# Weaving two chunks of each weight tile column by column, so that TensorE loads its weights with a step of two

## The chip, the cores and the metric

The kernel runs on one core of a Trainium2 chip. The metric is the time of one execution in device microseconds; the number quoted for a kernel is the median of its runs. Beside the timed runs there is one profiled execution, whose trace gives every instruction's start, duration and engine; all durations below come from that one.

## What is computed

Two layers (DEPTH = 2) of a diffusion backbone work on 256 latent tokens and 256 context tokens of width 1024. A layer is a half-step SwiGLU feed-forward block, a token mixer (neighbourhood attention, a recurrent unit and a Fourier mix behind one input projection, and one output projection), and a second feed-forward block. Each is modulated by vectors made from `silu(c) @ w_ada`, and followed by a residual and a LayerNorm. Cut to what matters here:

```python
def swiglu(h, wg, wu, wd):
    return (jax.nn.silu(h @ wg) * (h @ wu)) @ wd

def ffn_sublayer(xs, m, j, wg, wu, wd, g, b):
    y = MACARON * swiglu(modulate(xs, m, j), wg, wu, wd)
    return residual_post_norm(xs, m[3 * j + 2] * y, g, b)

# token mixing: one projection in, three head groups, one projection out
q, k, v, xr, gr, f = jnp.split(h_lat @ w_in, cuts, axis=-1)
y_lat = jnp.concatenate([na_lat, lru_lat, fno_lat], axis=-1) @ w_out
```

All of it is float32. Nearly all of the arithmetic is `h @ weight`: gate and up projections of 1024 x 2816, the down projection of 2816 x 1024 (twice in a layer), the projections in and out of the mixer.

## The kernel before

**The products.** Activations stand transposed: 128 channels on the partitions, 512 tokens (256 context, 256 latent) along the free dimension. A matmul holds a 128 x 128 block of weights in the array and streams 256 tokens past it. For float32 accuracy from the faster `float32r` format every operand is split in two: a rounded high part and the rest as a low part. A product is then three matmuls: high weights times high activations, low weights times high, high weights times low. In the names, `whi` and `wlo` are the two parts of a weight tile; `hH`, `hL` and `aH`, `aL` those of the activations.

**A weight unit.** The weights come in units of 128 output columns and up to 8 chunks of 128 input rows. A unit is one tile of 128 partitions and 1024 columns, chunk after chunk: column `k * 128 + s` is output column `s` of chunk `k`. A down projection is cut into groups of 8, 7 and 7 chunks (`GROUPS`), so its second and third group have units of 7 chunks, 896 columns. The DMA that SyncE issues fills `raw` (5 buffers), ScalarE (ACT) rounds `raw` to `whi` in one copy (`use_one`, line 274), and VectorE (DVE), or GpSimd (POOL) for a listed part of the units, writes `wlo = raw - whi` (`split_lo`, line 591). `whi` and `wlo` have 5 buffers each. The last units before a norm go another way: in `later` they are kept as four quarters of 256 columns, and each quarter is split when there is room (in `piece` at line 637 and in `norm_latent` at line 660).

**The matmuls.** `proj_start` (lines 402 to 436) walks over the chunks: for chunk `k` it takes the block `kk_(h_, k)` of `whi` and `kk_(l_, k)` of `wlo`, 128 neighbouring columns each, and calls `mmh` (line 391), which issues one matmul for each 256 tokens. Every matmul instruction loads its own weights, so the trace has one weight load (LDWEIGHTS, on the row PEld) for each matmul (on PE), and the load for the next one runs while the present one streams:

```python
def kk_(t, k):
    return t[:, k * 128:(k + 1) * 128]
```

**What sets the order.** `advance` splits units ahead of their use (`LOOK = 5`), in one fixed order for the whole program; DVE also does the adaLN products (`acc`, lines 298 to 304), the residuals, the norms and parts of the attention. In the mixer the order is a list written out by hand (`ORDER`). The tiny matmuls `adat` (line 332) turn the adaLN sums into columns between two units of a feed-forward block.

Of the kernel before, what the change touches and what calls it, by code (L numbers as in the profile page):

```python
# [65 lines left out]
def kernel(ctx: ExitStack, tc: tile.TileContext, x, cx, vecs, cst, bias, w_ada,  # L66
# [15 lines left out]
    V, S, G, PE = nc.vector, nc.scalar, nc.gpsimd, nc.tensor  # L82
# [65 lines left out]
    for l in range(DEPTH):  # L148
        p = {}
# [66 lines left out]
    later = []  # L216
    lazy = object()
# [42 lines left out]
    def needs_ctx(l, b):  # L260
        return l == 0 or b < 10

    def use_one(eng=None):
        i = ptr["use"]
        it = seq[i]
        t = raw.pop(i)
        if it[0] in "bx":
            kept[it] = t
        elif it[0] == "w":
            n = units[it[1]][1] * 128  # L270
            h_ = whi_p.tile([128, 1024], F32R, tag="whi", name="whi")
            l_ = wlo_p.tile([128, 1024], F32R, tag="wlo", name="wlo")
            if eng is not lazy:
                S.copy(h_[:, :n], t[:, :n])  # L274
            if eng is None and it[1] in pool_lo:
                eng = G
            if eng is later or eng is lazy:
                for a, b in ((q * n // 4, (q + 1) * n // 4) for q in range(4)):
                    later.append((l_[:, a:b], t[:, a:b], h_[:, a:b], G) + (eng is lazy) * (0,))
            else:  # L280
                split_lo(l_[:, :n], t[:, :n], h_[:, :n], eng)
            hi[it[1]], lo[it[1]] = h_, l_
        elif it[0] == "a":
            _, l, b, kp = it
            nst = 2 if needs_ctx(l, b) else 1
            if kp == 0:
                acc[l, b] = acc_p.tile([128, 2, 512], F32, tag="acc", name="acc")
            a = acc[l, b]
            half = [slice(0, 64), slice(64, 128)]
            if kp == 3 and nst == 2:  # L290
                acc[l, b] = acc_p.tile([128, 2, 512], F32, tag="acc", name="fold")
            for kk in range(2):
                k = kp * 2 + kk
                for st in range(nst):
                    sc_ = scol[:, k, st:st + 1]
                    if k == KD - 1 and nst == 2:
                        for i, p in enumerate(half):
                            V.scalar_tensor_tensor(out=acc[l, b][half[st], i], in0=t[p, 512:], scalar=sc_[p],  # L298
                                                   in1=a[p, st], op0=ALU.mult, op1=ALU.add)
                        continue  # L300
                    if k == 0:
                        V.tensor_scalar(out=a[:, st], in0=t[:, :512], scalar1=sc_, scalar2=None, op0=ALU.mult)
                    else:
                        V.scalar_tensor_tensor(out=a[:, st], in0=t[:, kk * 512:(kk + 1) * 512], scalar=sc_,  # L304
                                               in1=a[:, st], op0=ALU.mult, op1=ALU.add)
            if kp == 3:
                pend_red.append([l, b, 0, None])
        else:
            _, l, b, kp = it
            if kp == 0:  # L310
                acc[l, b] = dps("adap")

            for kk in range(2):
                k = kp * 2 + kk
                PE.matmul(acc[l, b][32 * (k % 4):32 * (k % 4) + 32, :], lhsT=scol_z[:, k, :],
                          rhs=t[:, kk * 512:(kk + 1) * 512], start=(k < 4), stop=(k >= 4))
            if kp == 3 and l:
                pend_rows.append([l, b, None])
        ptr["use"] += 1
        if not own_room(it):  # L320
            ptr["raw"] -= 1
        issue()
# [67 lines left out]
        for i, c in enumerate(halves):  # L390
            PE.matmul(o[:, c], lhsT=w, rhs=X[:, k, c], start=first and i == 0, stop=last and i == len(halves) - 1)  # L391

    def kk_(t, k):
        return t[:, k * 128:(k + 1) * 128]


    def proj(us, tiles, X, c0, c1, order=None):
# [4 lines left out]
    def proj_start(us, tiles, X, late_w=False):  # L402
# [4 lines left out]
        def go(ks, c0, c1, i0=0, i1=len(us)):  # L407
            c = [slice(a, min(a + 256, c1)) for a in range(c0, c1, 256)]
            for k in ks:
                if late_w:  # L410
                    for i, ((h_, l_), o) in list(enumerate(zip(ws, tiles)))[i0:i1]:
                        n = done[c0, i] = done.get((c0, i), 0) + 1
                        mmh(o, kk_(h_, k), X[0], k, c, n == 1, False)
                        mmh(o, kk_(h_, k), X[1], k, c, False, False)
                        mmh(o, kk_(l_, k), X[0], k, c, False, n == nk)
                    continue
                high(k, c0, c1)
                low(k, c0, c1)

        def high(k, c0, c1):  # L420

            c = [slice(a, min(a + 256, c1)) for a in range(c0, c1, 256)]
            n = done[c0, "h"] = done.get((c0, "h"), 0) + 1
            for (h_, l_), o in zip(ws, tiles):
                mmh(o, kk_(h_, k), X[0], k, c, n == 1, False)
                mmh(o, kk_(l_, k), X[0], k, c, False, False)

        def low(k, c0, c1):
            c = [slice(a, min(a + 256, c1)) for a in range(c0, c1, 256)]
            n = done[c0, "l"] = done.get((c0, "l"), 0) + 1  # L430
            assert n <= done[c0, "h"]
            for (h_, l_), o in zip(ws, tiles):
                mmh(o, kk_(h_, k), X[1], k, c, False, n == nk)

        go.high, go.low = high, low
        return go
# [974 lines left out]
```

## Time and profile before

| what | value |
|---|---|
| runs shown | 1807.26, 1807.67, 1811.6 us; median 1807.67 us |
| the profiled execution's own time | 1805.85 us |
| its span, first to last instruction | 1804.1 us |
| mean granted clock of TensorE | 0.982 |
| PE busy | 1722.3 us, 95% of the span, 14241 matmuls |
| PEld busy (weight loads) | 1667.0 us, 92%, 14241 loads |
| DVE, ACT, POOL busy | 1227.6 us (68%), 699.9 us (39%), 324.7 us (18%) |

How to read it: PE busy is the time in which some matmul was under way. Matmuls are pipelined, so one matmul's duration (some 280 ns) is much longer than the distance from its start to the next one's start (some 115 ns). That distance is called the *pace* below. A busy PE can therefore still become quicker, if its pace falls; and what the pace is, is read from the count of matmuls in a stretch or from their starting times, never from the durations.

### The profile page before, as it was taken

The page shows a single profiled execution, that of the slowest core. Times are in us where ns is not written, and L with a number is a line of the kernel's source. Part 1 is how long each engine was busy: PE and PEld are TensorE (multiplying, and loading weights), DVE is VectorE, ACT ScalarE, POOL GpSimd, SP SyncE. Part 2 cuts the span into 40 slices and gives each one's busy share as a digit, 9 for nine tenths or more (in the row PEclk, how much of TensorE's full clock was granted, in tenths as well). Part 3 has the DMA queues.
Part 4 walks back from the last instruction along what each step waited for, and adds up shares of the span by engine and source line. Part 5 has one row for each costly group of instructions (what it writes and reads, how often), then busy time and mean ns, then how long its engine had stood idle before and what let it go on. Part 6 is the DMA issues. An engine that isn't in the chain of part 4 may idle for free.

```text
span 1804.1 us, 33865 instructions
## 1 busy us (share of the span) xinstructions
PE 1722.3 (95%) x14241; PEld 1667.0 (92%) x14241; DVE 1227.6 (68%) x1867; ACT 699.9 (39%) x1119; POOL 324.7 (18%) x258
## 2 busy tenths in 40 slices
PE   7999999998899999999999999999999988979997
PEld 5999999998788999999999999999999967869997
DVE  3799899847586488765664568855653768676565
ACT  2222222225756554312222363222222566655443
POOL 0132121215441062000000140000000556150000
PEclk9999999999999999999999999999999989989998
DMA  8565555632223125544444326565653233267662
GB/s 274 181 205 179 168 172 171 175 96 83 68 62 93 55 86 172 176 141 138 132 146 123 95 70 197 168 186 169 181 173 89 81 94 88 89 177 205 181 196 84
DMA packets 375080, 253.33 MB, mean 140 GB/s; under 512 B 8144, under 2 KB 336336, under 8 KB 374928
## 3 DMA queue, kind: packets, MB, share of 16 engines
q1 hardware_dynamic: 373856, 248.81, 46.6%
q8 instruction: 112, 1.84, 0.4%
q0 software_dynamic: 1072, 2.36, 0.4%
q14 instruction: 40, 0.33, 0.1%
HBM read 250.09 MB, written 1.05 MB: 139 GB/s over the span
## 4 chain that ended last, share of the span: by engine, by line
PE 76%; DVE 16%; ACT 4%; issue 3%; DMA 0%; POOL 0%; SPq 0%; DVEq 0%; ACTq 0%
PE gu L391 41%; PE dn L391 19%; PE head L391 5%; PE pj L391 3%; DVE acc L304 2%; PE wo L391 2%; PE adat L332 1%; DVE wlo L591 1%; DVE ri L903 1%; PE o L1097 1%; DVE xT L718 1%; DVE s L460 1%; DVE xl L870 1%; DVE fold L298 1%; ACT whi L274 1%
## 5 line engine op out<-in xcount | busy, mean ns | idle before, releaser
L391 PE MATMUL gu<-hH,whi 128*128 128x256 f32 x2336 | 494.7, 281 | 1.8 <-ACT hH L1262 1.8
L391 PE MATMUL gu<-hH,wlo 128*128 128x256 f32 x2336 | 491.7, 280 | 1.7 <-DVE wlo L591 1.7
L391 PE MATMUL gu<-hL,whi 128*128 128x256 f32 x2336 | 492.1, 280 | 1.0 <-DVE hL L591 0.9
L274 ACT CAST whi<-raw 128x1024 fp32r<-128x1024 f32 (+1 forms) x319 | 319.1, 1025 | 273.4 <-PE dn L391 97.6
L591 POOL TENSOR_TENSOR wlo<-raw,whi 128x1024 fp32r<-128x1024 f32 (+2 forms) x106 | 204.2, 1933 | 1174.8 <-ACT whi L274 1154.3
L391 PEld LDWEIGHTS gu<-hH,whi 128*128 128x128 f32 x2336 | 371.9, 190 | 5.7 <-ACT hH L1262 2.4
L391 PEld LDWEIGHTS gu<-hL,whi 128*128 128x128 f32 x2336 | 370.8, 190 | 1.6 <-DVE hL L591 1.6
L391 PEld LDWEIGHTS gu<-hH,wlo 128*128 128x128 f32 x2336 | 370.0, 189 | 2.2 <-DVE wlo L591 2.2
L591 DVE TENSOR_TENSOR wlo<-raw,whi 128x1024 fp32r<-128x1024 f32 (+1 forms) x245 | 297.7, 1218 | 92.2 <-ACT whi L274 89.3
L391 PE MATMUL dn<-aH,whi 128*128 128x256 f32 x1280 | 283.5, 281 | 1.6 <-DVE xT L718 1.6
L391 PE MATMUL dn<-aL,whi 128*128 128x256 f32 x1280 | 281.0, 279 | 0.0
L391 PE MATMUL dn<-aH,wlo 128*128 128x256 f32 x1280 | 280.8, 279 | 0.0
L304 DVE SCALAR_TENSOR_TENSOR acc<-raw,scol,acc 128x512 f32<-128x512 f32 x337 | 273.9, 860 | 1.0
L731 ACT CAST aH<-pr 128x512 fp32r<-128x512 f32 (+1 forms) x88 | 50.0, 568 | 420.8 <-DVE pr L730 420.8
L391 PEld LDWEIGHTS dn<-aH,whi 128*128 128x128 f32 x1280 | 207.5, 189 | 2.1 <-DVE xT L718 2.0
L391 PEld LDWEIGHTS dn<-aL,whi 128*128 128x128 f32 x1280 | 207.7, 189 | 0.0
L391 PEld LDWEIGHTS dn<-aH,wlo 128*128 128x128 f32 x1280 | 207.1, 188 | 0.1
L730 DVE TENSOR_TENSOR pr<-sg,gu 128x512 f32<-128x512 f32 (+1 forms) x84 | 51.6, 614 | 136.9 <-PE gu L391 131.9
L718 DVE SCALAR_TENSOR_TENSOR xT<-dn,gate,xT 128x256 f32<-128x256 f32 x174 | 78.0, 478 | 82.8 <-PE dn L391 82.4
L391 PE MATMUL pj<-hH,whi 128*128 128x256 f32 x384 | 84.0, 287 | 5.5 <-ACT pt L1066 2.8
L729 ACT ACTIVATE sg<-gu 128x512 f32<-128x512 f32 (+1 forms) x84 | 45.2, 538 | 107.5 <-PE gu L391 107.3
L391 PE MATMUL pj<-hH,wlo 128*128 128x256 f32 x384 | 82.7, 283 | 0.0
(239 smaller groups left out, 2129.0 us busy)
## 6 DMA issues: line engine op xcount, KB each, us to landing
raw<-in_w_ada_dram SPq DMA_DIRECT2D x136, 512.0 KB, 4.7
raw<-in_ff_gate_dram SPq DMA_DIRECT2D x88, 512.0 KB, 4.4
raw<-in_ff_up_dram SPq DMA_DIRECT2D x88, 512.0 KB, 4.8
raw<-in_ff_down_dram SPq DMA_DIRECT2D x64, 448.0 KB, 4.4
raw<-in_w_in_dram SPq DMA_DIRECT2D x36, 512.0 KB, 3.9
raw<-in_ff_down_dram SPq DMA_DIRECT2D x32, 512.0 KB, 4.7
raw<-in_w_out_dram SPq DMA_DIRECT2D x16, 512.0 KB, 4.1
in<-in_w_ada_dram SPq DMA_DIRECT2D x8, 512.0 KB, 6.9
```

The costliest lines, as they stand in the source:

```text
L274: S.copy(h_[:, :n], t[:, :n])
L298: V.scalar_tensor_tensor(out=acc[l, b][half[st], i], in0=t[p, 512:], scalar=sc_[p], in1=a[p, st], op0=ALU.mult, op1=ALU.add)
L304: V.scalar_tensor_tensor(out=a[:, st], in0=t[:, kk * 512:(kk + 1) * 512], scalar=sc_, in1=a[:, st], op0=ALU.mult, op1=ALU.add)
L332: PE.matmul(tp[:, q * 2:q * 2 + 2], lhsT=a[:, q * 128:(q + 1) * 128], rhs=w, start=True, stop=True)
L391: PE.matmul(o[:, c], lhsT=w, rhs=X[:, k, c], start=first and i == 0, stop=last and i == len(halves) - 1)
L460: (e1 or V).tensor_tensor(out=s1, in0=a, in1=z, op=ALU.add)
L591: (eng or V).tensor_tensor(out=dst_l, in0=src, in1=dst_h.bitcast(F32), op=ALU.subtract)
L718: V.scalar_tensor_tensor(out=xT[:, j, a:b], in0=ps[:, a:b], scalar=gate[:, st, j:j + 1], in1=xT[:, j, a:b], op0=ALU.mult, op1=ALU.add)
L729: S.activation(out=sg[:, c], in_=gp[:, c], func=AF.Silu)
L730: V.tensor_tensor(out=pr[:, c], in0=sg[:, c], in1=up[:, c], op=ALU.mult)
L731: S.copy(aH[:, m, c], pr[:, c])
L870: V.scalar_tensor_tensor(out=t3[:, :, off:], in0=s3[:, :, :256 - off], scalar=w[tp], in1=t3[:, :, off:], op0=ALU.mult, op1=ALU.add)
```

## The change

`in_order` and `woven` view 256 columns of a tile (two chunks `t = 0, 1` of 128 columns `s`) in two ways: with the two chunks one after the other, as `raw` has them, and with their columns alternating. `whi` and `wlo` are written through the second view, so that column `s` of chunk `2j + t` stands at `256 j + 2 s + t`. The DMA and `raw` stay as they are; ACT, DVE and POOL write (and DVE and POOL also read `whi`) with a step of two elements. `kk_` then takes every second column of a pair: 128 columns with a step of two, which reach over 1024 bytes of a partition instead of 512. A unit of 7 chunks has an odd chunk left; it keeps its 128 neighbouring columns, and it is copied and split by an instruction of its own (`in_pieces` gives two pieces, of 768 and 128 columns).

```diff
+    def in_order(t, a, b):
+        return t[:, a:b].rearrange("p (k t s) -> p k t s", t=2, s=128)
+
+    def woven(t, a, b):
+
+        return t[:, a:b].rearrange("p (k s t) -> p k t s", t=2, s=128)
+
+    def in_pieces(n):
+
+        e = n // 256 * 256
+        out = [(lambda t: in_order(t, 0, e), lambda t: woven(t, 0, e))]
+        if e < n:
+            out.append((lambda t: t[:, e:n],) * 2)
+        return out
+
     def use_one(eng=None):
...
             if eng is not lazy:
-                S.copy(h_[:, :n], t[:, :n])
+                for src, dst in in_pieces(n):
+                    S.copy(dst(h_), src(t))
...
                 for a, b in ((q * n // 4, (q + 1) * n // 4) for q in range(4)):
-                    later.append((l_[:, a:b], t[:, a:b], h_[:, a:b], G) + (eng is lazy) * (0,))
+                    later.append((woven(l_, a, b), in_order(t, a, b), woven(h_, a, b), G) + (eng is lazy) * (0,))
             else:
-                split_lo(l_[:, :n], t[:, :n], h_[:, :n], eng)
+                for src, dst in in_pieces(n):
+                    split_lo(dst(l_), src(t), dst(h_), eng)
...
-    def kk_(t, k):
-        return t[:, k * 128:(k + 1) * 128]
+    def kk_(t, k, nk):
+        if k == nk - 1 and nk % 2:
+            return t[:, k * 128:(k + 1) * 128]
+        return t[:, k // 2 * 256:(k // 2 + 1) * 256].rearrange("p (s t) -> p t s", t=2)[:, k % 2]
...
-                        mmh(o, kk_(h_, k), X[0], k, c, n == 1, False)
-                        mmh(o, kk_(h_, k), X[1], k, c, False, False)
-                        mmh(o, kk_(l_, k), X[0], k, c, False, n == nk)
+                        mmh(o, kk_(h_, k, nk), X[0], k, c, n == 1, False)
+                        mmh(o, kk_(h_, k, nk), X[1], k, c, False, False)
+                        mmh(o, kk_(l_, k, nk), X[0], k, c, False, n == nk)
```

`high` and `low` pass `nk` in the same way. The order of the work on every engine stays; 64 copies on ACT, 54 subtractions on DVE and 10 on POOL come in, one for each unit of 7 chunks. On ACT, at the end of the first feed-forward block's second group of gate and up projections (`sg` and `aH` are that block's activation, `whi` the weights' high part), there stood before:

```order
50 L729 ACTIVATE sg<-gu 128x512
51 L731 CAST aH<-pr 128x512
52 L274 CAST whi<-raw 128x1024 x2
53 L729 ACTIVATE sg<-gu 128x512
54 L731 CAST aH<-pr 128x512
55 L274 CAST whi<-raw 128x1024
56 L274 CAST whi<-raw 128x896
57 L729 ACTIVATE sg<-gu 128x512
```

and there stands now:

```order
50 L748 ACTIVATE sg<-gu 128x512
51 L750 CAST aH<-pr 128x512
52 L290 CAST whi<-raw 128x4x2x128 x2
53 L748 ACTIVATE sg<-gu 128x512
54 L750 CAST aH<-pr 128x512
55 L290 CAST whi<-raw 128x4x2x128
56 L290 CAST whi<-raw 128x3x2x128
57 L290 CAST whi<-raw 128x128
58 L748 ACTIVATE sg<-gu 128x512
```

Every copy of a whole unit has become one woven copy; the copy of 896 columns has become two. On DVE, in the same block between the adaLN products (`acc`, `fold`) and the product of the gate (`pr`), there stood before:

```order
187 L298 SCALAR_TENSOR_TENSOR fold<-raw,scol,acc 64x512 x4
188 L591 TENSOR_TENSOR wlo<-raw,whi 128x896
189 L325 TENSOR_TENSOR mcol_105<-adat,vT 128x2x4
190 L730 TENSOR_TENSOR pr<-sg,gu 128x512
191 L1211 TENSOR_SCALAR k_r<-k_r 128x8
```

and there stands now:

```order
187 L315 SCALAR_TENSOR_TENSOR fold<-raw,scol,acc 64x512 x4
188 L610 TENSOR_TENSOR wlo<-raw,whi 128x3x2x128
189 L610 TENSOR_TENSOR wlo<-raw,whi 128x128
190 L342 TENSOR_TENSOR mcol_105<-adat,vT 128x2x4
191 L749 TENSOR_TENSOR pr<-sg,gu 128x512
192 L1230 TENSOR_SCALAR k_r<-k_r 128x8
```

One subtraction has become two, and nothing else has moved. The line numbers are 16 to 19 higher in the changed kernel.

## Rows read from the trace of the kernel before

**Rows 1.** Page: busy time, share of the span and instructions of each engine.

```profile
PE 1722.3 (95%) x14241; PEld 1667.0 (92%) x14241; DVE 1227.6 (68%) x1867; ACT 699.9 (39%) x1119; POOL 324.7 (18%) x258
```

**Rows 2.** Page: the chain that ended last, its shares by engine.

```profile
PE 76%; DVE 16%; ACT 4%; issue 3%; DMA 0%; POOL 0%; SPq 0%; DVEq 0%; ACTq 0%
```

**Rows 3.** Users of `whi`: count, duration ns min/median/max, first and last start, forms.

```profile
L391 PEld LDWEIGHTS gu<-hH,whi x2336: 186/188/338, 29.4 to 1769.8; 128*128 128x128 f32 x195
L391 PE MATMUL gu<-hH,whi x2336: 276/281/583, 29.4 to 1770.0; 128*128 128x256 f32 x195
...
L391 PE MATMUL dn<-aH,whi x1280: 276/281/471, 140.9 to 1790.6; 128*128 128x256 f32 x183
...
L391 PE MATMUL pj<-hH,whi x384: 276/278/550, 460.5 to 1555.2; 128*128 128x256 f32 x192
...
L391 PE MATMUL head<-hH,whi x256: 276/281/579, 435.9 to 1452.3; 128*128 128x256 f32 x128
...
L391 PE MATMUL wo<-aH,whi x144: 276/281/388, 602.1 to 1590.4; 128*128 128x256 f32 x144
```

**Rows 4.** Groups, 1627 to 1770 us: busy us, mean ns of one | idle before.

```profile
L391 PE MATMUL gu<-hH,whi 128*128 128x256 f32 x302 | 83.4, 276 | 0.0
L391 PEld LDWEIGHTS gu<-hH,whi 128*128 128x128 f32 x301 | 56.5, 188 | 0.0
```

**Rows 5.** The same groups, 811 to 866 us.

```profile
L391 PE MATMUL gu<-hH,whi 128*128 128x256 f32 x156 | 31.1, 281 | 0.0
L391 PEld LDWEIGHTS gu<-hH,whi 128*128 128x128 f32 x156 | 24.1, 190 | 0.0
```

**Rows 6.** Stretches, L391 alone: length, PE busy (x), PEld busy (x), clock, DMA share, GB/s.

```profile
811.00:866.00 55.00, 55.00 (x469) 55.00 (x469) 1.00 0.46 139
...
1627.00:1770.00 143.00, 143.00 (x1264) 143.00 (x1264) 1.00 0.66 191
```

**Rows 7.** Timeline of PEld: start us, us, instruction, count.

```profile
366.23 0.97 PEld L332 LDWEIGHTS adat<-pick,fold 128*128 128x128 f32 x8
```

**Rows 8.** Timeline of PE: eight records of transposes of `xT`.

```profile
1539.05 1.03 PE L1064 MATMUL ptp<-cs,xT 128*128 128x128 f32 x8
```

**Rows 9.** Timeline of PE: score matmuls with 512 streamed columns.

```profile
1467.84 0.39 PE L1005 MATMUL sc<-k,q 128*128 128x512 f32 x1
1468.07 0.39 PE L1006 MATMUL sc<-k,q 128*128 128x512 f32 x1
1468.30 0.39 PE L1005 MATMUL sc<-k,q 128*128 128x512 f32 x1
```

**Rows 10.** Groups by form, whole span: the splitting of weights, and two shorter subtractions.

```profile
L274 ACT CAST whi<-raw 128x1024 fp32r<-128x1024 f32 x255 | 260.8, 1047 | 235.3 <-PE dn L391 93.7 <-DMA raw<-in_ff_gate_dram 54.2 <-DMA raw<-in_ff_down_dram 31.6
L591 DVE TENSOR_TENSOR wlo<-raw,whi 128x1024 fp32r<-128x1024 f32 x191 | 236.4, 1241 | 71.8 <-ACT whi L274 69.3 <-issue 2.0
...
L274 ACT CAST whi<-raw 128x896 fp32r<-128x896 f32 x64 | 58.9, 940 | 38.1 <-DMA raw<-in_ff_down_dram 28.0 <-PE dn L391 3.9 <-PE adat L332 3.1
...
L591 DVE TENSOR_TENSOR aL<-pr,aH 128x512 fp32r<-128x512 f32 x66 | 45.0, 686 | 6.3 <-ACT aH L731 6.2
...
L591 DVE TENSOR_TENSOR aL<-pr,aH 128x256 fp32r<-128x256 f32 x22 | 9.2, 420 | 1.6 <-ACT aH L731 1.4
...
L591 POOL TENSOR_TENSOR wlo<-raw,whi 128x1024 fp32r<-128x1024 f32 x60 | 153.3, 2564 | 425.1 <-ACT whi L274 404.6 <-DVE mod L575 8.7 <-DVE k_r L1209 8.5
...
L591 POOL TENSOR_TENSOR wlo<-raw,whi 128x256 fp32r<-128x256 f32 x36 | 28.5, 798 | 7.0 <-ACT whi L274 7.0
```

**Rows 11.** Groups on DVE: one reads with a step of two, one without.

```profile
L325 DVE TENSOR_TENSOR mcol<-adat,vT 128x8 f32<-128x8 f32 x32 | 5.2, 163 | 89.1 <-PE adat L332 89.1
...
L1209 DVE TENSOR_TENSOR k_r<-k_r,k_z 128x8 f32<-128x8 f32 x8 | 1.3, 168 | 0.3
```

**Rows 12.** Stretch of the fullest DVE: length, PE, PEld, DVE, ACT, POOL, clock, DMA.

```profile
60.00:240.00 180.00, 176.47 (x1505) 175.90 (x1504) 162.91 (x237) 45.77 (x56) 44.16 (x25) 0.99 0.60 179
```

**Rows 13.** The same stretch, users of `wlo` alone: PE, PEld, DVE, POOL.

```profile
60.00:240.00 180.00, 96.60 (x486) 74.44 (x486) 22.81 (x17) 37.78 (x14) 0.99 0.60 179
```

More of the change, by code (lines that the diff above doesn't have):

```diff
@@ L424, in high @@
             for (h_, l_), o in zip(ws, tiles):
-                mmh(o, kk_(h_, k), X[0], k, c, n == 1, False)
-                mmh(o, kk_(l_, k), X[0], k, c, False, False)
+                mmh(o, kk_(h_, k, nk), X[0], k, c, n == 1, False)
+                mmh(o, kk_(l_, k, nk), X[0], k, c, False, False)
         def low(k, c0, c1):
@@ L432, in low @@
             for (h_, l_), o in zip(ws, tiles):
-                mmh(o, kk_(h_, k), X[1], k, c, False, n == nk)
+                mmh(o, kk_(h_, k, nk), X[1], k, c, False, n == nk)
         go.high, go.low = high, low
```

## The prediction

> **What bounds the kernel now.** I read the busy table first. PE has a matmul under way for 1722.3 of 1804.1 us [rows 1], so only some 82 us of the span are free of matmuls. The chain that ended last agrees: 76% of it is PE, 16% DVE, 4% ACT [rows 2]. So the time is the number of matmuls times their pace, plus a little waiting for DVE and ACT.
>
> The number comes from the users of `whi`. Each of the five products has three matmul groups of equal count (high-high, low-high, high-low), of which the high-high row is shown: 3 x (2336 + 1280 + 384 + 256 + 144) = 13,200 matmuls on line 391 [rows 3]. Those are the ones that the change touches. One nanosecond of their pace is 13.2 us, 0.7% of the time.
>
> The pace is read from stretches without a break. Between 1627 and 1770 us there are 1264 matmuls in 143 us; with the two or three that the edges cut taken off, that is 113.3 ns each. Between 811 and 866 us there are 469 in 55 us, 117.8 ns each in the same way [rows 6]. [...] It is the same instruction, of the same shape; its recorded duration is 276 ns in the fast stretch [rows 4] and 281 ns in the slow one [rows 5], so the duration tells which pace a matmul ran at. For `gu`, `dn`, `head` and `wo` the median is 281, for `pj` 278 [rows 3]: a little over half run at the slow pace. I take 52%, a mean pace of 0.52 x 117.8 + 0.48 x 113.3 = 115.6 ns.
>
> The weight loads differ too: 188 ns in the fast stretch, 190 ns on average in the slow one [rows 4, 5]. Something makes loads and matmuls late together.
>
> **How near the weight load is to the bound.** Eight loads in a row for the tiny `adat` matmuls, which stream two columns only, take 0.97 us; taking off one load's 0.19, (0.97 - 0.19) / 7 = 111 to 112 ns from load to load [rows 7]. So the load alone would hold the pace at about 112 ns: the fast pace is one nanosecond above it. The transposes, plain fp32 instructions with a load each, show what is possible below that: (1.03 - 0.27) / 7 = 109 ns [rows 8], the 0.27 being their duration.
>
> **The change part by part.** (1) *The load with a step of two.* The trace has no such load, so I bound its effect by the nearest rows. Gain: the lowest pace of any full matmul here is 109 ns [rows 8], so at most 13,200 x (115.6 - 109) = 87 us. Loss: if the load has to fetch twice as much and the part that grows with the columns doubles, 112 ns become up to 224, and 13,200 x (224 - 115.6) = 1.43 ms come on top. No row excludes that. I take a value at the gain's end, near the fast pace, for this reason. There are two stable paces for the same work at the same clock, the slow one with loads that are late as well: the two streams of reads of TensorE (256 columns of activations, 1024 bytes of each partition, and 128 columns of weights, 512 bytes) disturb each other. They go through memory in the same time, so now the activations' addresses move twice as fast as the weights'. With a step of two the 128 weights reach over 1024 bytes also, and the two streams move alike; two streams at one speed need not meet again and again. I expect the slow pace to go, and what is left to lie between the load's own 112 and the fast 113.3: 112.7 ns. That gives 13,200 x (115.6 - 112.7) = 38 us.
>
> (2) *Weaving on ACT, DVE and POOL.* From 1024 and 896 columns, 1047 and 940 ns, a copy on ACT costs 0.84 ns for each column and 0.19 us besides; 64 more copies are 12 us of an engine that is 39% busy [rows 1, 10]. On DVE, 512 and 256 columns at 686 and 420 ns give 0.15 us besides [rows 10]: 54 x 0.15 = 8 us. On POOL, 1024 and 256 columns at 2564 and 798 ns give 0.2 us: 10 x 0.2 = 2 us, 18% busy. PE's matmuls cover ACT and POOL altogether, since units are split up to five ahead. DVE has little room only from 60 to 240 us, 162.9 of 180 us busy [rows 12]; I charge 2 us for what comes through there and in the norms. Whether steps of two make these engines slower for each column is not shown at size: the one row in which DVE reads with a step of two has 8 elements, 163 ns against 168 without [rows 11], which speaks for no cost, and I take none. Bound: if every column cost twice as much, the 17 subtractions of that stretch, 22.8 us now [rows 13], would take some 18 us more, and DVE would need 181 us of 180; so up to 20 us could come through there. In the other direction these engines can't gain: they do the same columns in the same or more instructions.
>
> (3) *Waits.* None is added. A matmul of an even chunk waits for the piece with its pair, which is at most as large as the whole unit was; the odd chunk waits for an instruction behind it, and it is the last to be used. DMAs and their order stay. If PE becomes 38 us faster, weights are wanted 2% sooner: the stretch from 60 to 240 us has 1505 matmuls, would lose 4 us, and DVE's 163 us still fit into 176.
>
> Sum, against the profiled execution: 1805.85 - 38 + 2 = 1770 us. The runs' median is 1.8 us (0.1%) above that execution; I leave it there. No change means within 0.3%, 5.4 us, about what a measurement of this kernel can tell.
>
> **The rivals.** *A. Nothing changes on PE.* The two paces could belong to the stream of activations alone. [...] Against it speaks that the loads of the slow stretch are late too [rows 4, 5]. Time: 1805.85 + 2 = 1808.
>
> [...]
>
> *B. More goes than the slow pace.* If the excess of both paces comes from the two streams, and the load's 112 comes from the same source, the pace falls to 109: 1805.85 - 87 + 2 = 1721 us. For it: plain fp32 instructions run at 109 beside their loads. [...]
>
> *C. The load becomes the bound (slower).* The load is the mechanism, on PEld, under every one of the 13,200 matmuls. Its 112 ns have 1.3 ns of room under the fast pace; every nanosecond more than that is exposed. With a step of two a load reaches over twice as many bytes. If it becomes 5 ns slower, nearly the step between the two paces, it comes to 117 and every matmul runs at the slow pace or a little above, 117.8: 13,200 x (117.8 - 115.6) = 29 us, with the 2 us of weaving 1837 us. From 3.6 ns on (112 to 115.6) the change is a loss. For it: the small room. Against it: nothing in the trace shows a step to cost anything, at 8 elements. The far end of the load's bound, more than 3 ms, belongs here too.
>
> [...]
>
> That the change doesn't do what it says can be left out: the 128 columns of a load are the same values in either layout, and each matmul loads its own.
>
> **How the numbers follow.** Forecast 0.34, A 0.20, B 0.17, C 0.29 (of which 0.05 for the far end and 0.05 for weaving that costs more than I took). Faster by over 0.3%: forecast and B, 0.51. Within 0.3%: 0.20. Slower: 0.29. The time is the forecast's, 1770. The range goes from B, with a few microseconds below it, 1715, to C, 1840: it leaves out the far end and half of what is left of C above it, about 0.12, and 0.05 below. The forecast's own range, paces of 112 to 113.3 with 0 to 4 us of weaving, is 1758 to 1780.
>
> **What would show it.** Right: line-408 matmuls with one duration only, 276 ns or less, in all stretches; some 488 starts in an unbroken 55 us where there were 469; 128-column pieces of 0.3 us on ACT and DVE; ACT's woven copies at 1047 ns and DVE's at 1241. Rival A: 276 and 281 still side by side. B: durations near 272, a pace of 109. C: loads longer than 192 ns in long unbroken stretches. It would be wrong above all if the step changes the pace in a way that neither of the present two paces shows.

## The result, and the profile after

The changed kernel takes 1854.28 us (median of 4 runs, 1852.91 to 1854.96) against 1807.47 us (4 runs): a ratio of 1.0256, 95% interval [1.0234, 1.0277]. It is 2.6% slower. The prediction was 1770 us with a range to 1840, so both its sign and its range failed.

The busy table and the chain's shares of the profile after, the profiled execution of 1854.79 us with a span of 1853.0:

```profile
PE 1777.2 (96%) x14241; PEld 1723.3 (93%) x14241; DVE 1231.9 (66%) x1921; ACT 731.9 (40%) x1183; POOL 333.7 (18%) x268
PE 79%; DVE 14%; ACT 3%; issue 3%; DMA 1%; SPq 0%; DVEq 0%; ACTq 0%
```

The count of matmuls is that of [rows 1], and PE is busy 54.9 us longer. The time free of matmuls fell from 81.8 to 75.8 us. So nothing waits longer than before: all of the loss, and 6 us more, is in the pace of the matmuls themselves, on the engine on which the chain lies.

Stretches of the profile after, line 408 alone; the columns are those of [rows 6]:

```profile
831.00:887.00 56.00, 56.00 (x470) 56.00 (x468) 1.00 0.46 137
1666.00:1823.00 157.00, 157.00 (x1311) 157.00 (x1310) 1.00 0.62 179
```

With the two or three that the edges cut taken off, that is 119.9 ns from start to start in both, at a granted clock of 1.00, as there. The stretch that ran at 113.3 in [rows 6] and the one that ran at 117.8 now run alike, and slower than either. Averaged over every two starts on that line that are less than 140 ns apart (some 12,880), the pace went from 115.7 to 119.9 ns; times 13,200 that is 55 us, about what PE's busy time gained.

The groups by form that answer to [rows 3, 10], whole span (busy us, mean ns of one | idle before):

```profile
L408 PE MATMUL gu<-hH,whi 128*128 128x256 f32 x2336 | 504.1, 285 | 1.9 <-ACT hH L1281 1.8
L408 PEld LDWEIGHTS gu<-hH,whi 128*128 128x128 f32 x2336 | 382.7, 196 | 5.8 <-ACT hH L1281 2.5 <-issue 1.7 <-ACT hH L622 1.7
...
L290 ACT CAST whi<-raw 128x1024 fp32r<-128x1024 f32 x255 | 284.6, 1143 | 236.7 <-PE dn L408 96.3 <-DMA raw<-in_ff_gate_dram 45.1 <-DMA raw<-in_ff_down_dram 30.6
...
L290 ACT CAST whi<-raw 128x128 fp32r<-128x128 f32 x64 | 18.9, 295 | 0.0
...
L610 DVE TENSOR_TENSOR wlo<-raw,whi 128x1024 fp32r<-128x1024 f32 x191 | 236.4, 1241 | 77.4 <-ACT whi L290 74.5 <-issue 2.4
...
L610 DVE TENSOR_TENSOR wlo<-raw,whi 128x128 fp32r<-128x128 f32 x54 | 15.6, 289 | 0.0
```

The mean weight load is now 196 ns over the whole span. In the stretch from 831 to 887 us it is 194, where the slow stretch of before had 190 [rows 5]:

```profile
L408 PEld LDWEIGHTS gu<-hH,whi 128*128 128x128 f32 x156 | 24.3, 194 | 0.0
```

ACT's woven copy takes 1143 ns where the straight one took 1047 [rows 10]; DVE's subtraction takes 1241 in either layout, and POOL's 2609 where it took 2564. The last chunk of an odd unit goes in pieces of 0.3 us on ACT and DVE.

### The profile page after: what moved, and what is told of

Its sections match the earlier page's. It is cut to its first block, busy times and chain, and to the rows that moved or that the text cites. A ratio compares the mean times of both kernels' runs of the same rounds, so it can differ in the third digit from the quotient of the medians.

```text
span 1853.0 us, 33996 instructions
## 1 busy us (share of the span) xinstructions
PE 1777.2 (96%) x14241; PEld 1723.3 (93%) x14241; DVE 1231.9 (66%) x1921; ACT 731.9 (40%) x1183; POOL 333.7 (18%) x268
## 4 chain that ended last, share of the span: by engine, by line
PE 79%; DVE 14%; ACT 3%; issue 3%; DMA 1%; SPq 0%; DVEq 0%; ACTq 0%
PE gu L408 41%; PE dn L408 21%; PE head L408 5%; PE pj L408 3%; PE wo L408 2%; DVE acc L321 2%; PE adat L349 1%; DVE ri L922 1%; PE o L1116 1%; DVE s L479 1%; DVE wlo L610 1%; DVE xT L737 1%; ACT whi L290 1%; PE gate L898 1%; DVE xl L889 1%
## 5 line engine op out<-in xcount | busy, mean ns | idle before, releaser
L408 PE MATMUL gu<-hH,whi 128*128 128x256 f32 x2336 | 504.1, 285 | 1.9 <-ACT hH L1281 1.8
L408 PE MATMUL gu<-hH,wlo 128*128 128x256 f32 x2336 | 500.3, 283 | 2.0 <-DVE wlo L610 2.0
L408 PE MATMUL gu<-hL,whi 128*128 128x256 f32 x2336 | 500.6, 283 | 1.2 <-DVE hL L610 1.1
L290 ACT CAST whi<-raw 128x1024 fp32r<-128x1024 f32 (+2 forms) x383 | 352.0, 962 | 273.1 <-PE dn L408 100.8
L610 POOL TENSOR_TENSOR wlo<-raw,whi 128x1024 fp32r<-128x1024 f32 (+3 forms) x116 | 213.7, 1852 | 1203.3 <-ACT whi L290 1155.2
L408 PEld LDWEIGHTS gu<-hH,whi 128*128 128x128 f32 x2336 | 382.7, 196 | 5.8 <-ACT hH L1281 2.5
L408 PEld LDWEIGHTS gu<-hH,wlo 128*128 128x128 f32 x2336 | 382.7, 195 | 2.4 <-DVE wlo L610 2.4
L408 PEld LDWEIGHTS gu<-hL,whi 128*128 128x128 f32 x2336 | 383.2, 196 | 1.7 <-DVE hL L610 1.7
L610 DVE TENSOR_TENSOR wlo<-raw,whi 128x1024 fp32r<-128x1024 f32 (+2 forms) x299 | 301.5, 1025 | 97.3 <-ACT whi L290 93.9
L408 PEld LDWEIGHTS dn<-aH,wlo 128*128 128x128 f32 x1280 | 213.7, 194 | 0.1
```

What stands on the lines that cost most here:

```text
L290: S.copy(dst(h_), src(t))
L610: (eng or V).tensor_tensor(out=dst_l, in0=src, in1=dst_h.bitcast(F32), op=ALU.subtract)
```

## The experiments

Kernels that consist of blocks of matmuls, and nothing of the reference, are called benches. In a bench `W` holds the weights, `X` the stream, and the 256-column blocks go to X's two halves in turn, as the kernel does.

**Reading alone, and weaving alone.** Two kernels take the change apart. The first is the kernel before with the new loads and no weaving, so that each product mixes the columns of two neighbouring chunks:

```diff
-    def kk_(t, k):
-        return t[:, k * 128:(k + 1) * 128]
+    def kk_(t, k, nk):
+        if k == nk - 1 and nk % 2:
+            return t[:, k * 128:(k + 1) * 128]
+        return t[:, k // 2 * 256:(k // 2 + 1) * 256].rearrange("p (s t) -> p t s", t=2)[:, k % 2]
```

> The kernel before with the loads' step of two alone: the tiles are not woven, so each load takes every second column of a pair of neighbouring chunks (the products mix two chunks' weights; order and amount of work are unchanged). If the step of the loads makes the whole difference: 1852 to 1856 us, pace 120.0 in unbroken stretches. If weaving has a part of the 47 us: 1807.5 plus the rest, for instance 1840 if ACT's 100 ns more for each copy come through.

Measured: 1850.78 us, ratio 1.0238 [1.0218, 1.0258]. The second is the changed kernel with that function put back, so that the tiles are woven and the loads straight (its products, too, mix the columns of two chunks):

> The changed kernel with loads of 128 neighbouring columns again: the tiles are woven by ACT, DVE and POOL as in the change, but read straight (the products take the wrong columns; the amount of work is unchanged). If the step of the loads makes the whole difference: 1805 to 1810 us, paces of 113 and 118 side by side as before. If weaving costs time: over 1813 us, with longer waits of PE for whi and wlo.

Measured: 1809.21 us, ratio 1.0009 [0.9998, 1.002]. One unbroken stretch of the first and two of the second, their products' line alone:

```profile
1666.00:1822.00 156.00, 156.00 (x1303) 156.00 (x1303) 1.00 0.62 180
```

```profile
894.00:950.00 56.00, 56.00 (x496) 56.00 (x495) 1.00 0.53 161
1625.00:1778.00 153.00, 153.00 (x1301) 153.00 (x1300) 1.00 0.64 184
```

Reading with a step gives the 120 ns of the changed kernel (156 / 1301). Weaving alone keeps the two paces of before, 113.3 and 117.8, though not in the same stretches: the long one that was fast is now slow. The loads' step makes the loss, within the two intervals; weaving is hidden.

**The load's step in a bench.** Blocks of 96 matmuls, in which the step of the weights and the streamed columns differ:

```python
if step == 1:
    w = W[:, k * 128:k * 128 + cols]
else:
    b = (k // step) * 128 * step % 1024
    w = W[:, b:b + cols * step].rearrange("p (s t) -> p t s", t=step)[:, k % step]
```

> A kernel of its own: nothing but blocks of 96 float32r matmuls from one tile of weights and one of activations, each block with another step of the weights (1, 2, 3, 4, 8), width of the weights (128, 64, 32 columns), number of streamed columns (16, 256, 384, 512) and step of the streamed columns (1, 2); it leaves out the whole of the reference. Three theories. [...] (2) The load is the bound: the pace with 16 streamed columns, where nothing else takes time, is 112 at step one and 120 at step two, and at 384 and 512 streamed columns the step changes nothing. (3) The stream has its own excess: with 64 or 32 weight columns the pace at 256 stays 113 or more, and at 512 it is 226 or more whatever the step; step two then adds something that isn't in the stream.

The timeline of PE, start us and us (the digits at a name's end are left out by the trace: w1, w2 and so on is the step, the shape tells the streamed columns):

```profile
26.41 11.68 PE L56 MATMUL w1n<-X,W 128*128 128x256 f32 x96
37.93 11.68 PE L56 MATMUL w2n<-X,W 128*128 128x256 f32 x96
49.45 17.15 PE L56 MATMUL w3n<-X,W 128*128 128x256 f32 x96
66.44 22.57 PE L56 MATMUL w4n<-X,W 128*128 128x256 f32 x96
88.85 23.33 PE L56 MATMUL w8n<-X,W 128*128 128x256 f32 x96
112.01 21.95 PE L56 MATMUL w1n<-X,W 128*128 128x512 f32 x96
133.80 22.57 PE L56 MATMUL w2n<-X,W 128*128 128x512 f32 x96
...
272.76 16.81 PE L56 MATMUL w1n<-X,W 128*128 128x384 f32 x96
289.40 16.80 PE L56 MATMUL w2n<-X,W 128*128 128x384 f32 x96
```

From start to start of two blocks, by 96: step one 120.0, two 120.0, three 177, four 233, eight 241 ns. So the load does pay for its step, steeply from three on, where the pace is far above the 120.0 of straight loads behind the same 256 columns. But at 256 columns straight loads ran at 120.0 as well, a third pace that no long unbroken stretch of before had, so the bench did not repeat the 113.3 and could not price a step of two. Behind 384 columns the two steps are equal, 173.3; behind 512 they are not: 227.0 without a step and 233.3 with one, although PEld is idle for part of the time there (busy for 36.40 of 44 us from 112 to 156, over the two blocks). So a longer stream does not hide the step in every case.

Two of the blocks with straight loads of only 32 columns, which take 108 ns each on average (those of 128 columns 192):

```profile
250.60 11.06 PE L56 MATMUL w1c32n<-X,W 128*32 128x256 f32 x96
...
438.61 11.47 PE L56 MATMUL w1c32n<-X,W 128*32 128x256 f32 x96
```

They ran at 113.3 and at 117.8 ns, the two paces of the kernel before. So neither pace needs a load of 128 columns, and 256 streamed columns took 113.3 ns even beside a load a quarter as wide. The blocks of 16 columns, meant to show the load alone, fell to a granted clock of 0.50 and said nothing: a miss.

**The load alone.** The same in shorter blocks between wide ones, at a granted clock of 1.00, and blocks in which the weights begin some columns further:

```python
SHORT = [(f"s{s}n{n}y", s, n, 16, "W", 0) for n in (16, 64, 128, 192, 224) for s in (1, 2, 4)]
```

> A second kernel of blocks of matmuls (the reference is left out whole). Four plain fp32 matmuls of two columns, like adat, stand as a break before each block of 256 or 512 streamed columns, ten times for step one and step two; short blocks of 16 matmuls with 16 to 224 streamed columns stand between full ones, so that the clock stays up; the last blocks take weights from a tile 64 KB further off, or from 1 to 32 columns later. Theory of two streams: a load with a step of two has no room left in its reading, and the activations' stream hardly any, so that they disturb each other only while both run: with 64 or 128 streamed columns step one and step two both take about 112 ns, at 256 step two takes 120 and step one 113, 118 or 120 by the phase that the break leaves, at 512 it is 227 against 233, at 320 the step makes 0 to 7 ns. Rival, the load alone is the bound: at 64 and 128 streamed columns step two takes 120 ns, and at 320, 448 and 512 the step makes no difference. Rival, the memory's place: blocks with the far tile or a later first column have another pace than those of the same step at the old place.

The timeline of PEld (16 loads, behind 16 and 128 streamed columns), then that of PE behind 320 columns and with the weights 1, 2, 4 and 16 columns on (`o1`, `o2`, `o4`, `o16`):

```profile
304.96 1.88 PEld L62 LDWEIGHTS s1n16y<-X,W 128*128 128x128 f32 x16
312.50 1.96 PEld L62 LDWEIGHTS s2n16y<-X,W 128*128 128x128 f32 x16
320.13 3.81 PEld L62 LDWEIGHTS s4n16y<-X,W 128*128 128x128 f32 x16
...
356.97 1.88 PEld L62 LDWEIGHTS s1n128y<-X,W 128*128 128x128 f32 x16
364.51 1.97 PEld L62 LDWEIGHTS s2n128y<-X,W 128*128 128x128 f32 x16
```

```profile
567.12 5.92 PE L62 MATMUL s1n256o1z<-X,W 128*128 128x256 f32 x48
573.69 5.80 PE L62 MATMUL s1n256o2z<-X,W 128*128 128x256 f32 x48
580.14 5.92 PE L62 MATMUL s1n256o4z<-X,W 128*128 128x256 f32 x48
...
593.28 5.71 PE L62 MATMUL s1n256o16z<-X,W 128*128 128x256 f32 x48
...
637.71 7.28 PE L62 MATMUL s1n320z<-X,W 128*128 128x320 f32 x48
645.64 7.29 PE L62 MATMUL s2n320z<-X,W 128*128 128x320 f32 x48
```

Taking off one load's mean duration (192 ns for step one, 196 for two, 329 for four) and dividing by 15, a load follows a load after 112.5 ns with a step of one, 117.6 with two, 232 with four. Behind 16 streamed columns there is next to no stream to meet, and behind 128 it is the same: these are the load's own rates. The step of two costs 5 ns by itself, and the load with it needs more than the 115.6 ns of the mean matmul before. Behind 320 columns the step costs next to nothing (7.28 and 7.29 us for 48 matmuls). A load that has become too long for 256 columns is rival C's mechanism. The `o` blocks brought something else: one and the same straight load runs at 118.3, 115.6 or 113.3 ns as its place moves (5.71 against 5.92 us of 48 matmuls).

The same bench moved the weights with a step of two as well, by 4, 8 and 32 columns:

```profile
606.22 5.95 PE L62 MATMUL s2n256o4z<-X,W 128*128 128x256 f32 x48
...
619.47 6.06 PE L62 MATMUL s2n256o32z<-X,W 128*128 128x256 f32 x48
```

By the starts inside the blocks these are 118.6, 120.0 and 121.1 ns. So the pace with a step of two moves with the place too, and here stays above the 117.6 of the load alone.

**Wider matmuls.** If the load is the bound only because 256 columns are just as long, one matmul of 512 columns per load hides it. The kernel before and the changed one, with

```diff
-            c = [slice(a, min(a + 256, c1)) for a in range(c0, c1, 256)]
+            c = [slice(a, min(a + 512, c1)) for a in range(c0, c1, 512)]
```

in all three places:

> The kernel before with one matmul of 512 streamed columns where there were two of 256 (where both token streams are projected at once), so half of the loads there, each with 128 neighbouring columns. By the blocks measured before, 226.7 ns for 512 columns against a mean of 2 x 115.6 = 231.2: with some 5,000 pairs 20 to 25 us less, 1780 to 1788 us. If the excess belongs to the stream alone and its phase, as the score matmuls' 226 to 236 ns would have it, the mean stays at 231 and the time at 1800 to 1808.

> The changed kernel with one matmul of 512 streamed columns where there were two of 256. Theory of two streams: 233.3 ns for 512 columns, which is less than 2 x 120.0 but over the 226.7 of step one: 6.7 ns more than the kernel with wide matmuls and straight loads in each of some 5,000, that is 30 to 35 us above it plus what the 256-column matmuls keep of the loss (4.4 ns in each of some 3,000, 13 us). If the load alone is the bound, it is hidden behind 512 columns, and only the 256-column matmuls lose: 10 to 15 us above it.

Measured: 1814.57 us, ratio 1.004 [1.0026, 1.0055], and 1813.95 us, 1.0034 [1.0022, 1.0046]. A stretch of 512-column matmuls in either (PE, PEld):

```profile
898.00:955.00 57.00, 57.00 (x246) 45.94 (x245) 1.00 0.54 157
```

```profile
893.00:949.00 56.00, 56.00 (x244) 47.17 (x243) 1.00 0.53 159
```

With half the loads, the loads no longer fill PEld (46 of 57 us), and the changed kernel is no slower than the other. Both expectations are misses, however. The kernel before with wide matmuls gains nothing: a 512-column matmul takes some 233 ns without a step (57 / 244.5), where twice 113.3 would be 226.7. The streamed columns have an excess of their own, which fewer loads don't remove. And the changed kernel, expected at least 10 us above it, lies level, though not because the step is simply hidden. Some 3,200 matmuls still have 256 columns, since only one of the two token streams is projected there, and in the changed kernel they still pay for it; its longest stretch of them ran at 119.9 ns, where the kernel before with wide matmuls ran at 117.8:

```profile
1626.00:1782.00 156.00, 156.00 (x1303) 156.00 (x1303) 1.00 0.63 180
```

Over the whole traces the 256-column matmuls go at 119.9 against 116.3 ns, some 12 us lost, and the 4,900 wide ones at 230.4 against 233.3, some 14 us gained; the two cancel. Behind 512 columns the step gained 3 ns in the kernel and cost 6 in the bench, and no run shows why.

**Place or phase.** One thing differs from block to block: the column at which the weights begin (w), the stream's (x), or a lone narrow matmul that shifts the first load against the first stream (p behind weight column 0, q behind column 16):

```python
CASES = [(f"w{w}o", 1, w, 0, 0) for w in (0, 8, 16, 24, 32, 48, 64, 96, 112, 128, 256, 272)]
CASES += [(f"x{x}o", 1, 0, x, 0) for x in (4, 16, 32, 48, 64)]
CASES += [(f"p{p}o", 1, 0, 0, p) for p in (6, 20, 50, 78, 110, 140)]
CASES += [(f"q{p}o", 1, 16, 0, p) for p in (6, 20, 50, 78, 110, 140)]
```

> Blocks of 64 matmuls of 256 streamed columns, each behind a pause; one thing differs from block to block: the column at which the weights begin (w0 to w272), the column at which the stream begins (x4 to x64), a lone matmul of 6 to 140 columns ahead that shifts the start of the first load against the first stream (p at weight column 0, q at weight column 16), all with a step of one; and with a step of two the lone matmul (r) and the weight column (t). It computes nothing of the reference. The block at weight column 0 went at 120 ns in the run before and the one at column 16 at 113.3. Theory (places): the pace of straight loads is set by where weights and stream lie: all p at 120, all q at 113.3, and moving the stream by 16 columns against the weights gives 113.3 as moving the weights did. Rival (phase): it is set by how far the load has got when the stream starts, and kept: the p and q blocks spread over 113.3, 117.8 and 120 whatever the column. Both: a load with a step of two never goes below 117.6 (its floor behind 16 streamed columns), so every r and t block lies between 117.6 and 121.

Timeline of PE (64 matmuls of 256 columns each):

```profile
46.31 7.92 PE L55 MATMUL w0o<-X,W 128*128 128x256 f32 x64
...
63.35 7.78 PE L55 MATMUL w16o<-X,W 128*128 128x256 f32 x64
...
80.19 7.83 PE L55 MATMUL w32o<-X,W 128*128 128x256 f32 x64
...
97.10 7.92 PE L55 MATMUL w64o<-X,W 128*128 128x256 f32 x64
...
156.66 7.78 PE L55 MATMUL x16o<-X,W 128*128 128x256 f32 x64
165.09 7.84 PE L55 MATMUL x32o<-X,W 128*128 128x256 f32 x64
...
242.75 7.52 PE L55 MATMUL q6o<-X,W 128*128 128x256 f32 x64
...
251.03 7.79 PE L55 MATMUL q20o<-X,W 128*128 128x256 f32 x64
```

From the starts inside the blocks: at distance 0, 64, 128 and 256 the pace is 120.0, whatever precedes; at 32 and 96 it is 118.6; at 16, 48, 112 and 272 it is 117.8; and at 16 behind a lone matmul of 6, 50 or 110 columns it is 113.3, behind one of 20, 78 or 140 it is 117.8 again. Moving the stream by 16 or 32 gives what moving the weights gives. So the *distance* of weights and stream, modulo 64 columns, sets which paces there are, and at distance 16 the phase chooses between two. My expectation that all q blocks run at 113.3 was wrong in that. All blocks of this bench with a step of two ran at 119.9 to 120.1.

The kernel before has just these two paces, so it should lie at distance 16 or 48. Padding of 64 bytes ahead of the weights' pools moves it by 16:

```diff
+    pad_p = ctx.enter_context(tc.tile_pool(name="pad", bufs=1))
     wraw = ctx.enter_context(tc.tile_pool(name="wraw", bufs=5))
...
+    G.memset(pad_p.tile([128, 16], F32, tag="pad", name="pad"), 0.0)
```

> The kernel before with 64 bytes of padding ahead of the weight tiles' pools, so that every weight tile lies 16 columns further from the streamed activations; nothing else changes, and the loads stay straight. Theory (places): the share of the slow pace falls or grows as a whole; with all 13,200 matmuls at 113.3 in place of 115.6 ns it gives 30 us, about 1777 us, with all at 118.5 it costs 38 us, about 1846 us. Rival (phase): the two paces stay mixed about half and half, and the time stays at 1803 to 1812 us.

```profile
1650.00:1805.00 155.00, 155.00 (x1309) 155.00 (x1308) 1.00 0.63 182
```

Measured: 1835.8 us, ratio 1.0145 [1.0121, 1.0168], and 118.6 ns in that stretch and all others, the pace of distance 32. So the kernel before lies at 16 (from 48, the padding would have led to distance 0 and 120.0), and nothing but 64 bytes of padding costs 26 us.

**The map, and the best place.** All 64 distances in two phases:

> Every distance of 0 to 63 columns between the first column of the weights and of the stream, modulo the 64 columns after which the run before repeated itself; 40 straight loads and streams of 256 columns each, behind a lone matmul of 6 and of 20 columns (two phases). It computes nothing of the reference. If the place sets the pace, distance 0 gives 120, distances 16 and 48 give 113.3 or 117.8 by the phase, distance 32 gives 118.6, distance 8 gives 118.4, whichever phase where only one pace is stable; a distance whose pace is below 115 in both phases would take a kernel with straight loads below 1800 us. If the phase alone did it, the paces would not follow the distance.

Timeline of PE, blocks of 40:

```profile
218.23 4.80 PE L50 MATMUL d16p6o<-X,W 128*128 128x256 f32 x40
...
223.79 4.96 PE L50 MATMUL d16p20o<-X,W 128*128 128x256 f32 x40
...
252.46 4.81 PE L50 MATMUL d19p6o<-X,W 128*128 128x256 f32 x40
...
258.03 4.79 PE L50 MATMUL d19p20o<-X,W 128*128 128x256 f32 x40
```

Paces, from the starts inside the blocks, reach from 113.3 (4.79 to 4.81 us) to 122.1. Only distances 13 and 19 had the fast pace in both phases (4.79 to 4.81 us in all four blocks). Two first tries to bring the kernel there went wrong, each in its own way. In one the four activation tiles were moved by 5 columns, and the weights by 8:

```diff
-    hH = const.tile([128, KD, 512], F32R, name="hH")
...
+    ha = const.tile([128, 4 * 4096 + 8], F32R, name="ha")
+    hH, hL, aH, aL = (ha[:, 5 + q * 4096:5 + (q + 1) * 4096].rearrange("p (k n) -> p k n", k=8) for q in range(4))
```

> The kernel before with its four activation tiles taken as slices of one tile, 5 columns in; with the 8 columns of padding the weights then lie 19 columns from the stream modulo 64 in place of 16. Nothing else changes, the loads stay straight. Theory (places): at distance 19 the map showed 113.3 ns in both phases, where at 16 it showed 113.3 or 117.8 by the phase; so every unbroken stretch goes at 113.3, 13,200 matmuls by 2.2 ns are 30 us, of which the shift by 16 showed some 70%: 1777 to 1787 us. Rival (phase): the mixture stays, 1803 to 1812 us; and if the writes to odd columns cost the other engines, slower than 1812 us.

> The changed kernel with the same shift by three columns. Theory (the load with a step of two is itself the bound, 117.8 ns even behind 16 streamed columns): no place brings it below 117.8, so with 118 to 120 ns it stays at 1835 to 1858 us. Rival (the step costs only because of the place): it falls with the kernel before, to 1777 to 1800 us.

Measured: 1875.32 us, ratio 1.0376 [1.0361, 1.039], and for the changed kernel moved in this way 1886.12 us, 1.0434 [1.0418, 1.0451]. Most long stretches of the first went at 123.3 ns, such as this one, and the others at 120.0:

```profile
927.00:987.00 60.00, 60.00 (x489) 60.00 (x488) 1.00 0.49 147
```

In the map the weights had been moved, here the stream. I had taken one to be as good as the other, from moves of 16 to 64 columns; for a stream that begins 5 columns in it was wrong. The other try made the ten weight buffers slices of one tile, handed out in a fixed turn, so that a tile could be overwritten while it was wanted; it changes which weights are multiplied, and its waits:

> The kernel before, with its ten weight buffers as slices of one tile that begin 3 columns in: now the weights are moved by three columns (distance 19) and the stream keeps its place, where the run before moved the stream off it. Theory (places; a stream that begins at a column that is no multiple of 4 pays for itself, a load does not): as in the map, 113.3 ns in both phases, so all unbroken stretches at 113.3 and 1777 to 1787 us. Rival (a shift by three columns costs whichever side has it, or the phase keeps both paces): 1803 us or more.

Measured: 1789.57 us, ratio 0.9897 [0.9877, 0.9917], two causes in one. The runs that settled it keep the turn of the buffers: high and low part of a unit share one buffer of 2112 columns (33 x 64, so that every buffer has the same distance), and a scratch buffer is given up for the room.

```diff
...
-            h_ = whi_p.tile([128, 1024], F32R, tag="whi", name="whi")
-            l_ = wlo_p.tile([128, 1024], F32R, tag="wlo", name="wlo")
+            w_ = whi_p.tile([128, 2112], F32R, tag="w", name="w")
+            h_, l_ = w_[:, 3:1027], w_[:, 1027:2051]
```

> The kernel before with high and low part of a weight tile in one buffer of 2112 columns, 3 columns in, so that the weights lie 19 columns from the stream modulo 64; one scratch buffer less makes room for the padding. Theory (place): all unbroken stretches at 113.3 ns, against 115.6 before: 30 us by 13,200 matmuls, of which the shift by 16 columns showed some 70%; 1780 to 1792 us, and 18 to 30 us below the next run. Rival (the last run's gain came from its buffers): no difference to the next run.

> The same without the three columns: distance 16 as in the kernel before. Both theories: the two paces of before mixed, 1803 to 1815 us; what it differs from the kernel before is the price of the paired buffers and of the scratch buffer.

> The changed kernel (woven pairs, loads with a step of two) with the weights at distance 19. Theory (the step itself is the cost, since the load alone takes 117.8 ns behind 16 streamed columns): no place helps it, 118 to 122 ns and 1835 to 1870 us. Rival (place): it falls to 1780 to 1800 us as the straight one does.

Measured: 1786.25 us, ratio 0.9878 [0.9861, 0.9896]; without the three columns 1809.17 us, 1.0005 [0.9996, 1.0015]; the changed kernel with them 1858.17 us, 1.0276 [1.026, 1.0292]. The same stretch of some 1310 matmuls in the three, in this order:

```profile
1602.00:1750.00 148.00, 148.00 (x1308) 148.00 (x1308) 1.00 0.67 191
```

```profile
1624.00:1778.00 154.00, 154.00 (x1310) 154.00 (x1309) 1.00 0.64 184
```

```profile
1670.00:1826.00 156.00, 156.00 (x1303) 156.00 (x1302) 1.00 0.62 180
```

113.4, 117.8 and 119.9 ns. The busy table and a group of the first:

```profile
PE 1694.5 (95%) x14241; PEld 1641.1 (92%) x14241; DVE 1224.3 (69%) x1867; ACT 700.2 (39%) x1119; POOL 327.3 (18%) x258
L390 PE MATMUL gu<-hH,w 128*128 128x256 f32 x4672 | 739.1, 278 | 3.9 <-DVE w L590 2.1 <-ACT hH L1261 1.8
```

With straight loads, three columns take 27.8 us off PE's busy time of [rows 1], and the kernel is 1.2% faster than the one before. With a step of two the same three columns gain nothing. So the slow pace of the straight loads is a matter of place, and what takes it away does not take away the loss by the step. The other distances were not tried with a step of two in the kernel.

## Why the prediction was wrong

**What bounds the kernel: right.** PE's matmuls are the path, 13,200 of them on one line, and a nanosecond of pace is worth about 13 us: 4.2 ns gave 55 us of busy time, and 2.1 ns less (113.6 on average with the weights at distance 19) gave 28. The two paces, the mean of 115.6 (115.7 over the whole trace) and the load's own 112 ns, read from eight `adat` loads [rows 7], were right too (112.5 in the bench).

**Part (1), the load with a step of two: the step that failed.** The argument was that weights and activations disturb each other because one stream moves at half the other's speed, and that "two streams at one speed need not meet again and again". From its bounds (109 to 224 ns) I took 112.7. Measured: 117.6 for the load alone and 120.0 under 256 columns. Half of the argument is true: the two streams do disturb each other, since the pace follows their distance in memory, between 113.3 and 122.1 with the same loads and streams. The false half is that a step of two only changes how they meet. The load itself becomes slower, by 5 ns where hardly anything streams (112.5 to 117.6 ns behind 16 columns), and 1.3 ns was all the room there was. I had the number for that room and the floor, put the load's own cost at nothing, and let a story on the interplay outweigh them. Nor was the 112.7 to be had by a better load: 256 streamed columns took 113.3 ns even beside loads of 32 columns. The load's new floor accounts for some 25 of the 55 us of busy time (115.7 to 117.6 ns); the other 2.3 ns, some 30 us, come when load and stream run together.

**Rival C: right in its mechanism as far as that goes, too small in its size.** It said that 5 ns more on the load bring it to 117 and every matmul to 117.8, a loss from 3.6 ns on. The load did go from 112.5 to 117.6. But beside 256 streamed columns matmuls come every 120.0 ns, so the loss was 47 us where I had 31. What lies between 117.6 and 120.0 moves with the place of the weights (118.6 to 121.1 in the bench of the load alone); what makes it stays open. Nor is the load's length the whole mechanism: in the bench a step of two cost 6 ns behind 512 columns too, where the load's own 117.6 ns left more than 100 of the 233 to spare.

In the benches the step's price is small at two and large from three on (behind 256 columns 120.0 ns at one and at two, 177 at three, 233 at four), but at two it is not nothing: a load takes 117.6 against 112.5 ns behind 16 columns, and nearly half of the loss follows from that 5%.

**Rival A: wrong.** The streamed columns have an excess of their own (233 ns for 512 columns in the wider kernel, where twice the fast pace is 226.7; the score matmuls of before came every 230 ns [rows 9]), but the load was no bystander: in the map nothing differs but the distance of weights and stream and the phase, and the pace goes from 113.3 to 122.1.

**Rival B: wrong**, with the forecast: no stretch and no block of 256-column matmuls with full loads came below 113.3 ns in any run. Its 109 ns were read from matmuls of another kind: the transposes stream 128 columns of plain fp32, and in the same trace 256 such columns (the `fy` matmuls, lines 958 and 959) come every 215 to 216 ns. So they are no bound for 256 columns here.

**Part (2), weaving: right in the time, wrong in one row.** I charged 2 us; weaving alone measured 1.0009 [0.9998, 1.002], so at most some 4 us. DVE writes woven columns at the old duration (1241 ns for 1024), as taken. ACT doesn't: 1143 against 1047 ns for 1024 columns, 24 us over 255 copies that I had at nothing, covered by PE's matmuls, with ACT busy for 40% of the span. POOL takes 2% longer for a woven unit. **Part (3)**, no new wait, held: PE's free time fell by 6 us.

**The signs I named.** Loads longer than 192 ns in long unbroken stretches were to show C, and they did (194 in both of the stretches shown). The last sentence, a pace that neither of the two paces shows, is what happened.

## What to carry to other kernels

Where the weight load and the stream are equally long, compare the load's own pace with the matmul's before anything is done to the load: here 1.3 ns of room stood against 5 ns of cost, 13,200 times. Two paces for one shape at one clock can be a matter of where the operands lie: move one of them by a few columns, as an experiment of its own, before redesigning the access; three columns were worth 1.2% here, and an unlucky padding of 64 bytes cost 26 us. Move the weights rather than the stream for that: a stream that began 5 columns in ran at 120.0 to 123.3 ns, where weights moved to the same distance gave 113.4. If a step of the load is needed, measure it with the matmuls as wide as they will be: in the benches it cost nothing behind 320 and 384 streamed columns and 6 ns behind 512.

## What the runs showed that I had not expected

- The pace of 256 streamed columns with straight loads takes values between 113.3 and 122.1 ns by the distance between weights and stream modulo 64 columns (256 bytes), and at some distances one of two by the phase. What in the memory repeats after 256 bytes was not shown.
- A load of 128 columns costs 112.5 ns with a step of one, 117.6 with two, 232 with four, load to load.
- A stream that begins 5 columns in ran at 120.0 to 123.3 ns, with the weights at a distance that gives 113.4 when the weights are moved in its place. No other odd start was tried.
- With a step of two the pace follows the place as well (118.6 to 121.1 ns at three places in one bench, 119.9 to 120.1 at all places of another), and behind 512 streamed columns the step cost 6 ns in a bench and gained 3 in the kernel.
